# The rank-16 product of the log decay: two fp32 passes over 16 rows, or one fp32r pass over 80 stacked rows

## The chip, the cores and the metric

The kernel runs on one core of a Trainium2 chip. The metric is device time in microseconds (us) of one execution; the time before is the median of three runs. The core has a matrix engine (PE, with its weight loads shown as PEld), a vector engine (DVE), an activation engine (ACT), a general engine (POOL) and a queue that issues DMAs (SP). Each works through its own instructions in order, and semaphores tie them together.

## What is computed

One encoder block over 16 meta tokens and 1024 sequence tokens with 1024 channels, in float32. A norm is followed by one wide projection, whose columns are split into eight parts. Two mixers run beside each other: a pooling mixer, and gated linear attention (GLA) with 4 heads in chunks of 64 tokens. Their outputs are weighted by sigmoid gates, summed and projected, and a squared-ReLU MLP and a last norm follow. What matters here is the log decay of GLA:

```python
z = jnp.einsum('bld,dn->bln', u, w_in)
a, q, k, v, r, lr, ga, gb = jnp.split(z, IN_SPLITS, axis=-1)
log_a = jax.nn.log_sigmoid((lr @ w_gate_up + b_gate).astype(jnp.float32)) / GLA_TAU
...
b = jnp.cumsum(ac, axis=2)
decay = jnp.exp(-jnp.abs(b[:, :, :, None, :] - b[:, :, None, :, :]))
scores = jnp.einsum('bhtk,bhsk,bhtsk->bhts', qc, kc, decay)
```

`lr @ w_gate_up` is a product of rank 16: for every token 16 numbers times a 16 x 256 matrix. The 256 results are the decay of 4 heads with 64 channels each.

## The kernel before, in words

**Number formats.** Large products are made from fp32r operands. Each float32 operand is split into a high part, made by an ACT copy into fp32r, and a low part, made by subtracting the high part on DVE or POOL. Three matrix passes then give high by high, high by low and low by high (`mm3`, lines 246 to 248). Small products take float32 operands as they are, and the PE runs each as two passes. The product of the log decay (`log_decay`, line 1073) is one of these.

**Stages.** (1) From the start to about 200 us: norm, transposes, the tile `lrtok` with the 16 columns of `lr` by token, and the gates in quarter blocks (`start`, `differences`, `gate_stage`). (2) To about 305 us: the pooling mixer, which ends with four `ya_block` steps that read the tile `pm` and write to `ma_dram`. (3) From 305 us: `gla_open` lays out the tiles of GLA, then `gla` runs. (4) From about 490 us: the outputs of GLA are merged and projected. (5) From about 630 us: the MLP, and the last norms with the output.

**The 16 columns.** `lr_turn` (line 508) turns `lrtok` on the PE: the meta tokens go to `lrT_meta` (16 x 16), the sequence to the first 16 rows of `gB` (16 x 1024). It is called in stage 1, between blocks that split the operands of the gates (`halved`, lines 708 and 709; `differ`, line 714). There the order on ACT, DVE and POOL is the program's. The weight `wgu` (16 x 256) is fetched at line 775 in stage 1.

**GLA.** Four units are worked on, (p, half) = (0,0), (1,0), (0,1), (1,1): a pair of heads by 512 tokens. Each unit begins in `inside` with `log_decay`: the product, then on ACT a bias, `Abs`, `Exp` and `Ln` in the tile `yt`, then one DVE instruction that writes `g`, and an `Exp` on `g` (line 1140). Then come seven groups of small score products (`scores`, line 1128); six of them follow a level of growing factors (`grow`, lines 1158 to 1162) and are taken into `scc` under a mask (line 1189). `across` follows one unit behind and ends with lines 1257 to 1260, which read the tile `mix`, of which `g` is a quarter. `meta_state` makes a `log_decay` of 16 tokens for p = 0 and for p = 1, just ahead of the units (0,0) and (1,0). Between these pieces the PE is given filler work: the k columns (`k_block`, evacuated at line 958), the second half of v, the rest of the gates gb, and the GLA output product.

**What sets the order.** The PE's order is the program's, everywhere. On ACT, DVE, POOL and SP a planner sets the order within the stages, by its own estimate of when things are ready, except in stage 1 and from the end of GLA into stage 4 (`in_order`), where ACT and DVE follow the program. Weights come through a ring (`Ring.top_up`): a DMA into a raw tile (line 101), the high part on ACT (line 77), the low part (line 78) on DVE, and on POOL during GLA.

**Memory.** Tiles are pushed onto two stacks, left and right. A new tile that takes the place of an old one waits until the old one's last reader is done. At `gla_open` the right stack keeps only its lowest tile (`vw1`, line 797); `pm` lay next above it.

Of the kernel before, what the change touches and what calls it, by code (L numbers as in the profile page):

```python
# [8 lines left out]
F32 = mybir.dt.float32  # L9
F32R = mybir.dt.float32r  # L10
U8 = mybir.dt.uint8
ACT = mybir.ActivationFunctionType
ALU = mybir.AluOpType
AX = mybir.AxisListType

P = 128
# [4 lines left out]
HALF = 512  # L21
# [84 lines left out]
def kernel(  # L106
# [3 lines left out]
    nc = tc.nc  # L110
# [3 lines left out]
    w_gate_up, b_gate, gla_norm, w_gla_out, w_out = w_gate_up[0], b_gate[0], gla_norm[0], w_gla_out[0], w_out[0]  # L114
    norm_ffn, w_ff1, w_ff2 = norm_ffn[0], w_ff1[0], w_ff2[0]

    act, dve, pool, pe = nc.scalar, nc.vector, nc.gpsimd, nc.tensor
    left, right = Stack(tc, "left"), Stack(tc, "right")
# [19 lines left out]
    def bank(tag):  # L138
        if tag in rota:
            turn_of[tag] = turn_of.get(tag, -1) + 1  # L140
            tag = rota[tag][turn_of[tag] % len(rota[tag])]
        return psp[tag].tile([P, 512], F32, name=f"b_{tag}", tag=tag)
# [20 lines left out]
    gB = left.push("gB", [P, D], F32)  # L163
# [10 lines left out]
    stat = [tiny(16) for _ in range(4)]  # L174
    eps_t = tiny(1)
    pool.memset(eps_t, EPS)
    wgu = left.push("wgu", [16, 256], F32)
    metab = left.push("metab", [P, 4, 16], F32)
    lrT_meta = left.push("lrT_meta", [16, 32], F32)[:, :16]
    raw = Raw(nc, [left.push(f"raw{i}", [P, D], F32) for i in range(2)])  # L180
    W1 = Ring(nc, raw, left.push("w1h", [P, 2, D], F32R), left.push("w1l", [P, 2, D], F32R), 2)
    left_ff = left.mark()
# [8 lines left out]
    def f32(ap):  # L191
        return ap.bitcast(F32)

    def col(v, n):
        return v.rearrange("(h p) -> p h", p=P)
# [54 lines left out]
    def quad(a):  # L250
        return a.rearrange("p (k c) -> p k c", k=4)
# [149 lines left out]
    S, rings = {}, [W1]  # L401
# [32 lines left out]
    def buffer(key, depth, size=HALF):  # L434
        S[key] = left.push(key, [P, depth, size], F32)
        S["n" + key], S["d" + key] = 0, depth
# [36 lines left out]
    def v_tile(i, t, later=False):  # L473
# [25 lines left out]
        def leave_lr():  # L499
            if i == 0:  # L500
                act.activation(S["lrtok"][:n, t], b[:, 256:], ACT.Copy)
# [3 lines left out]
        leave()  # L505
        leave_lr()

    def lr_turn():
        b = bank("ms")
        pe.transpose(b[:16, :16], S["lrtok"][:16, 8], ident[:16, :16])  # L510
        act.activation(lrT_meta, b[:16, :16], ACT.Copy)
        for h in range(2):
            b = bank("ms")
            for t in range(4):
                pe.transpose(b[:16, t * P : (t + 1) * P], S["lrtok"][:, 4 * h + t], ident)
            act.activation(gB[:16, h * HALF : (h + 1) * HALF], b[:16], ACT.Copy)
# [248 lines left out]
    def gate_stage():  # L765
        q = gate_quarters
        S["u3p"] = right.push("u3p", [P, 2, HALF], F32)
        buffer("t1", 3)
        buffer("o", 2)
        buffer("c", 2)  # L770
        q.room = True
        nc.sync.dma_start(pscale, col(pool_scale, 4))
        nc.sync.dma_start(bgate, col(b_gate, 2))
        nc.sync.dma_start(gnorm, col(gla_norm, 4))
        nc.sync.dma_start(wgu, w_gate_up)
        q.leaving = next_weights
        for _ in S["gate_run"]:
            pass
        rota["mm"] = ("mm", "mm", "x", "x")
# [7 lines left out]
    one = []  # L787
    step(one, start)
    step(one, gate_stage)


# [134 lines left out]
    def gla_open():  # L926
        raw.back()
        W1.eng = pool
        right.pop_to(1)
        left.pop_to(left0)  # L930
        S["kq"] = [left.push(f"kq{h}", [P, 2, 2, HALF + OFF[h]], F32) for h in range(2)]
        for h in range(2):
            q = S["kq"][h][:, :, 1, OFF[h] : OFF[h] + HALF]
            for p in range(2):
                nc.sync.dma_start(q[:, p], q_dram[p, h])
        S["v"].append(left.push("v1", [P, NC, 2 * P], F32))
        buffer("t1", 3)
        buffer("o", 3)

        mix = left.push("mix", [P, 4, HALF], F32)  # L940
        S["kt"], S["qe"], S["kl"], S["g"] = quad(mix[:, 0]), mix[:, 1], mix[:, 2], mix[:, 3]
        S["on"], S["sr"] = mix[:, 0:2].rearrange("p a (b c) -> p (a b) c", b=4), mix[:, 2:4]
        S["ends"] = left.push("ends", [P, HALF], F32)
        S["scc"] = left.push("scc", [P, 2, 2, 4, CH], F32)
        S["S"] = left.push("S", [P, 2, 2, P], F32)
        S["W"] = left.push("W", [P, NC - 1, P], F32)
        S["left_n"] = left.mark()
        S["N"] = [left.push(f"n{i}", [P, HALF, 2], F32) for i in range(2)]
        S["F"] = left.push("f", [P, HALF, 2], F32)
        S["yt"] = left.push("yt", [P, 2, HALF], F32)  # L950
        banks(keep=1, sc=1, m2=1, mx=1, ms=1)
        rota["mm"] = ("mm", "mm", "mx")

    step(one, gla_open)

    def k_block(p):
# [110 lines left out]
        step(fill, yb_block(j, 0), W1, [rows4(w_gla_out, j)])  # L1067


    def log_decay(lrT, p, n, dst, y, t, tag="ms"):  # L1070

        b = bank(tag)[:, :n]
        pe.matmul(b, wgu[:, p * P : (p + 1) * P], lrT, start=True, stop=True)
        act.activation(y, b, ACT.Identity, bias=bgate[:, p : p + 1])
        act.activation(t, y, ACT.Abs)
        act.activation(t, t, ACT.Exp, scale=-1.0)
        act.activation(t, t, ACT.Ln, bias=1.0)
        dve.scalar_tensor_tensor(dst, y, 0.0, t, ALU.min, ALU.subtract)
# [52 lines left out]
    def inside(p, half, before):  # L1131

        kq = S["kq"][half][:, p, :, OFF[half] : OFF[half] + HALF]
        N, F, scc, g, ends = S["N"], S["F"], S["scc"][:, p], S["g"], S["ends"]
        log_decay(gB[:16, half * HALF : (half + 1) * HALF], p, HALF, g, S["yt"][:, 0], S["yt"][:, 1])
        act.activation(g, g, ACT.Exp, scale=1.0 / TAU)  # L1140
        yield 4.5
        b = scores(kq[:, 0], kq[:, 1])
        act.activation(scc, b, ACT.Copy)
        pairs = lambda a: a.rearrange("p (b u) n -> p b u n", u=2)
        plain, gp = kq.rearrange("p n (b u) -> p b u n", u=2), g.rearrange("p (b u) -> p b u", u=2)
        for u, to, other in ((1, N[0], F), (0, F, N[0])):
            dve.tensor_tensor(
                pairs(to)[:, :, u], plain[:, :, u], gp[:, :, u : u + 1].broadcast_to([P, HALF // 2, 2]), ALU.mult
            )
            act.activation(pairs(other)[:, :, u], plain[:, :, u], ACT.Copy)  # L1150

        def grow(m, n, to, e, e2):

            b = HALF // (4 * m)
            outer = lambda a: bass.AP(a.tensor, a.offset, (a.ap[0], (8 * m, b), (6 * m, 2), (1, 2 * m)))
            inner = lambda a: bass.AP(a.tensor, a.offset + 2 * m, (a.ap[0], (8 * m, b), (2 * m, 2), (1, 2 * m)))
            over = lambda at, step: bass.AP(e.tensor, e.offset + at, (e.ap[0], (4, b), (step, 2), (0, 2 * m)))
            dve.tensor_tensor(outer(to), outer(n), over(1, 1), ALU.mult)
            act.activation(inner(to), inner(F), ACT.Copy)
            dve.tensor_tensor(inner(F), inner(n), over(0, 3), ALU.mult)  # L1160
            ev = e.rearrange("p (b u) -> p b u", u=2)
            dve.tensor_tensor(e2, ev[:, :, 0], ev[:, :, 1], ALU.mult)

        def last(n, e, e2):

            m = CH // 2
            ev = e.rearrange("p (b u) -> p b u", u=2)
            halves_of = lambda a: a.rearrange("p (b u m) -> p b u m", u=2, m=m)
            for i, o, u in ((0, S["kl"], 0), (1, S["qe"], 1)):
                a, f, o = halves_of(n[:, :, i]), halves_of(F[:, :, i]), halves_of(o)  # L1170
                dve.tensor_tensor(o[:, :, u], a[:, :, u], ev[:, :, 1 - u : 2 - u].broadcast_to([P, NC, m]), ALU.mult)
                act.activation(o[:, :, 1 - u], f[:, :, 1 - u], ACT.Copy)
            dve.tensor_tensor(e2, ev[:, :, 0], ev[:, :, 1], ALU.mult)

        yield 2.0
        e, at = g, 0
        for lvl in range(6):
            m, n = 1 << lvl, N[lvl % 2]
            to = at + HALF // (2 * m)
            e2 = ends[:, at:to]  # L1180
            if lvl < 5:
                grow(m, n, N[1 - lvl % 2], e, e2)
            else:
                while before and before not in done:
                    yield 0.8
                last(n, e, e2)
            e, at = e2, to
            b = scores(n[:, :, 0], n[:, :, 1])
            dve.copy_predicated(scc, mask[:, lvl : lvl + 1, None, :].broadcast_to([P, 2, 4, CH]), b)
            yield LEVEL  # L1190
# [487 lines left out]
```

## Time and profile before

| what | value |
| --- | --- |
| runs shown (us) | 1247.72, 1245.71, 1245.96 |
| median | 1245.96 us |
| profiled execution | span 1247.8 us from first to last instruction |
| PE busy | 1213.1 us, 97% of the span |
| DVE, ACT, POOL busy | 850.7, 615.4, 65.0 us |
| granted PE clock | 0.993 of full |

No separate time is given for the profiled execution, so its span stands for it; it is 1.8 us (0.15%) above the median of the runs and equal to the slowest of them. In the profile's rows "L1073" is line 1073 of the kernel, the bracket at the end of a row is idle time of the engine just before the instruction and what ended it, and "x2" means that the row stands for two instructions. A float32 product shows two weight loads and two matmuls, one of each for a pass.

### The profile page before, as it was taken

What the parts mean: (1) busy time and instruction counts of PE and PEld (TensorE: products, weight loads), DVE (VectorE), ACT (ScalarE), POOL (GpSimd) and SP (SyncE); (2) the same over time, 40 slices, a digit from 0 to 9 for tenths busy, and PEclk for the clock granted to TensorE, in tenths of its full rate; (3) what the DMA queues carried; (4) which work ended last, traced back from release to release, by engine and by line L of the source; (5) the groups of instructions that cost most, each with busy time, mean ns of one, the idle gap of its engine ahead of it and who ended that gap; (6) DMA issues with size and microseconds to landing.
All of it is one profiled execution on the core that took longest, in us unless ns stands there. A gap on an engine that the chain in (4) does not pass through costs nothing.

```text
span 1247.8 us, 18255 instructions
## 1 busy us (share of the span) xinstructions
PE 1213.1 (97%) x6822; PEld 1006.5 (81%) x6822; DVE 850.7 (68%) x1384; ACT 615.4 (49%) x1092; POOL 65.0 (5%) x70
## 2 busy tenths in 40 slices
PE   7999999999999999799999999999999999999997
PEld 6878888988887788688878888888887788888886
DVE  6897676653556677723897676766774777887786
ACT  6667567321446663412654554555553444444554
POOL 2100000001101115300000000000000000000000
PEclk9999999999999999899999999999999999999999
DMA  8033326156102246831234544544569773333432
GB/s 249 2 109 104 109 85 197 52 161 204 36 19 61 86 140 223 284 104 51 94 117 155 167 152 136 164 156 135 177 219 371 267 247 94 102 93 100 162 96 90
DMA packets 142682, 173.85 MB, mean 139 GB/s; under 512 B 10969, under 2 KB 82417, under 8 KB 142593
## 3 DMA queue, kind: packets, MB, share of 16 engines
q1 hardware_dynamic: 142592, 172.68, 42.8%
q8 instruction: 54, 0.88, 0.3%
q14 instruction: 36, 0.29, 0.1%
HBM read 119.17 MB, written 53.48 MB: 138 GB/s over the span
## 4 chain that ended last, share of the span: by engine, by line
PE 90%; DVE 5%; DMA 2%; issue 1%; ACT 1%; SPq 0%; DVEq 0%; ACTq 0%
PE b_mm L246 11%; PE b_mm L247 11%; PE b_mm L248 11%; PE b_ms L246 9%; PE b_ms L247 9%; PE b_ms L248 9%; PE b_x L246 8%; PE b_x L248 8%; PE b_x L247 8%; PE b_sc L1128 1%; PE b_mx L246 1%; PE b_mx L247 1%; PE b_mx L248 1%; PE b_ms L538 1%; DMA raw<-hf_dram 1%
## 5 line engine op out<-in xcount | busy, mean ns | idle before, releaser
L246 PE MATMUL b_mm<-th,w1h 128*128 128x512 f32 (+1 forms) x312 | 117.8, 378 | 3.2 <-ACT th L1385 2.1
L247 PE MATMUL b_mm<-tl,w1h 128*128 128x512 f32 (+1 forms) x312 | 116.0, 372 | 0.6 <-DVE tl L1386 0.6
L248 PE MATMUL b_mm<-th,w1l 128*128 128x512 f32 (+1 forms) x312 | 115.8, 371 | 0.0
L246 PE MATMUL b_x<-th,w1h 128*128 128x512 f32 (+1 forms) x240 | 90.8, 378 | 0.0
L247 PE MATMUL b_x<-tl,w1h 128*128 128x512 f32 (+1 forms) x240 | 90.6, 378 | 0.0
L248 PE MATMUL b_x<-th,w1l 128*128 128x512 f32 (+1 forms) x240 | 90.3, 376 | 0.0
L264 ACT ACTIVATE w1h<-raw 128x512 fp32r<-128x512 f32 x96 | 59.6, 621 | 36.7 <-PE b_x L247 14.1
L265 DVE TENSOR_TENSOR w1l<-raw,w1h 128x512 fp32r<-128x512 f32 x96 | 65.6, 684 | 12.3 <-ACT w1h L264 12.3
L246 PEld LDWEIGHTS b_mm<-th,w1h 128*128 128x128 f32 x312 | 58.5, 188 | 16.5 <-issue 3.3
L264 ACT ACTIVATE w1h<-fs 128x512 fp32r<-128x512 f32 x72 | 45.4, 631 | 46.4 <-PE b_ms L247 31.7
L247 PEld LDWEIGHTS b_mm<-tl,w1h 128*128 128x128 f32 x312 | 58.6, 188 | 10.5 <-DVE tl L1386 0.9
L248 PEld LDWEIGHTS b_mm<-th,w1l 128*128 128x128 f32 x312 | 58.6, 188 | 10.3
L264 ACT ACTIVATE w1h<-bt 128x512 fp32r<-128x512 f32 x44 | 27.8, 632 | 67.7 <-issue 59.5
L265 DVE TENSOR_TENSOR w1l<-fs,w1h 128x512 fp32r<-128x512 f32 x72 | 49.3, 685 | 14.7 <-ACT w1h L264 14.6
L1535 DVE TENSOR_TENSOR bt<-w,w 128x512 f32<-128x512 f32 x80 | 54.6, 683 | 0.4 <-DMA w<-in_w_ff_dram 0.4
L248 PEld LDWEIGHTS b_x<-th,w1l 128*128 128x128 f32 x240 | 45.1, 188 | 8.5
L246 PEld LDWEIGHTS b_x<-th,w1h 128*128 128x128 f32 x240 | 45.0, 188 | 8.4
L247 PEld LDWEIGHTS b_x<-tl,w1h 128*128 128x128 f32 x240 | 45.1, 188 | 8.2
L264 ACT ACTIVATE fxh<-bt 128x512 fp32r<-128x512 f32 x36 | 22.8, 632 | 57.6 <-issue 48.1
L246 PE MATMUL b_ms<-wo,w1h 128*128 128x512 f32 x128 | 49.8, 389 | 0.0
L247 PE MATMUL b_ms<-wo,w1h 128*128 128x512 f32 x128 | 49.8, 389 | 0.0
L248 PE MATMUL b_ms<-wo,w1l 128*128 128x512 f32 x128 | 49.8, 389 | 0.0
(438 smaller groups left out, 3370.2 us busy)
## 6 DMA issues: line engine op xcount, KB each, us to landing
hf_dram<-h SPq DMA_DIRECT2D x112, 256.0 KB, 2.1
raw<-hf_dram SPq DMA_DIRECT2D x112, 256.0 KB, 2.6
w<-in_w_ff_dram SPq DMA_DIRECT2D x64, 256.0 KB, 4.8
raw<-in_w_in_dram SPq DMA_DIRECT2D x24, 512.0 KB, 4.8
raw<-in_w_ff_dram SPq DMA_DIRECT2D x16, 512.0 KB, 4.1
rawx<-in_w_ff_dram SPq DMA_DIRECT2D x16, 512.0 KB, 4.0
xs<-in_x_dram SPq DMA_DIRECT2D x8, 512.0 KB, 4.9
rawx<-in_w_in_dram SPq DMA_DIRECT2D x8, 512.0 KB, 4.4
```

The lines of the kernel that those rows point to most:

```text
L246: pe.matmul(ps, ah, bh, start=first and i == 0, stop=False, skip_group_check=more)
L247: pe.matmul(ps, ah, bl, start=False, stop=False, skip_group_check=more)
L248: pe.matmul(ps, al, bh, start=False, stop=last and i == n - 1, skip_group_check=more)
L264: act.activation(hi, a, ACT.Copy)
L265: dve.tensor_tensor(lo, a, f32(hi), ALU.subtract)
L538: pe.transpose(b[j][:, i], u[:, (4 * j + i) * P : (4 * j + i + 1) * P], ident)
L1128: pe.matmul(b[to, e, j], kk[r, s], qq[r, s], start=True, stop=True, tile_position=(e * CH, u * CH))
L1535: dve.tensor_tensor(bt, w, S["w2"][q[3:]][:, i], ALU.add if q[2] == "+" else ALU.subtract)
```

## The change

The two operands of the product are stacked three times on partitions: the 16 rows of the tokens as (high, low, high) at partitions 0, 32 and 64, the 16 rows of the weight as (high, high, low) at the same partitions, and zeros on the rows between. One pass in fp32r over 80 rows then sums high by high, low by high and high by low.

```diff
-    wgu = left.push("wgu", [16, 256], F32)
+    wgu = left.push("wgu", [P, 256], F32R)
-    lrT_meta = left.push("lrT_meta", [16, 32], F32)[:, :16]
+    lrT_meta = left.push("lrT_meta", [P, 32], F32R)[:, :16]
...
+    RANK = 16
+    part_of = lambda a, i: a[32 * i : 32 * i + RANK]
+
+    def stacked(to, a, low):
+        pool.memset(f32(to[: 64 + RANK]), 0.0)
+        for i in range(3):
+            if i != low:
+                act.activation(part_of(to, i), a, ACT.Copy)
+        dve.tensor_tensor(part_of(to, low), a, f32(part_of(to, 0)), ALU.subtract)
+
     def lr_turn():
...
-        act.activation(lrT_meta, b[:16, :16], ACT.Copy)
+        stacked(lrT_meta, b[:16, :16], 1)
...
-        nc.sync.dma_start(wgu, w_gate_up)
...
         right.pop_to(1)
         left.pop_to(left0)
+        S["wgraw"] = right.push("wgraw", [RANK, 256], F32)
+        nc.sync.dma_start(S["wgraw"], w_gate_up)
+        stacked(wgu, S["wgraw"], 2)
...
-        S["yt"] = left.push("yt", [P, 2, HALF], F32)
+        S["y"] = left.push("y", [P, HALF], F32)
+        S["lr"] = left.push("lr", [P, HALF], F32R)
+        lr_of(0)
...
+    def lr_of(half):
+        stacked(S["lr"], gB[:RANK, half * HALF : (half + 1) * HALF], 1)
+
     def log_decay(lrT, p, n, dst, y, t, tag="ms"):
-        b = bank(tag)[:, :n]
-        pe.matmul(b, wgu[:, p * P : (p + 1) * P], lrT, start=True, stop=True)
+        b, k = bank(tag)[:, :n], slice(0, 64 + RANK)
+        pe.matmul(b, wgu[k, p * P : (p + 1) * P], lrT[k], start=True, stop=True)
...
-        log_decay(gB[:16, half * HALF : (half + 1) * HALF], p, HALF, g, S["yt"][:, 0], S["yt"][:, 1])
+        log_decay(S["lr"], p, HALF, g, S["y"], g)
+        if (p, half) == (1, 0):
+            lr_of(1)
```

The weight's DMA moves from stage 1 to `gla_open`, into a new tile `wgraw` on the right stack. The second half of the tokens is stacked into the same tile `lr` once unit (1,0) has read the first half. The two halves of `yt` become `y` and `lr`, and `Abs`, `Exp` and `Ln` are written into `g` itself.

## The prediction

> **What bounds the kernel now.** I read the page's chain first, then the busy time by stretches around the four units of GLA, then the order of time at each log-decay product. First the chain by engine (page), then four stretches: microseconds, and busy time of PE, PEld, DVE, ACT and POOL.
>
> ```profile
> PE 90%; DVE 5%; DMA 2%; issue 1%; ACT 1%; SPq 0%; DVEq 0%; ACTq 0%
> ```
>
> ```profile
> 305.00:317.00 12.00, 12.00 (x77) 10.92 (x76) 1.92 (x2) 3.71 (x6) 0.00 (x0) 1.00 0.15 57
> 317.00:345.00 28.00, 27.06 (x370) 23.26 (x372) 17.50 (x39) 14.30 (x29) 4.78 (x2) 1.00 0.16 40
> 345.00:375.00 30.00, 29.23 (x442) 25.95 (x435) 17.07 (x45) 11.33 (x26) 0.00 (x0) 1.00 0.07 20
> 388.00:428.00 40.00, 40.00 (x457) 31.24 (x456) 26.81 (x50) 27.05 (x46) 7.17 (x3) 1.00 0.29 87
> ```
>
> The PE is the path that sets the end for 90% of the span, and where the four products stand (317, 348, 388 and 428 us) it rests for 0.94 us of 28, 0.77 of 30 and nothing of 40. DVE and ACT are busy for 38 to 68% there. So a microsecond of PE work removed here should be a microsecond of the span, as long as nothing new makes the PE wait.
>
> **What the change removes: PE time.** The order of time on the PE around the product at 317 us (with the meta product ahead of it) and the one at 388 us; then the first and last row around those at 348 and 428 us; then, from the chain in order of time, eight narrow passes of an earlier stage.
>
> ```profile
> 316.92 0.28 PE L247 MATMUL b_mm<-tl,w1h 128*128 128x264 f32 x1
> 317.04 0.28 PE L248 MATMUL b_mm<-th,w1l 128*128 128x264 f32 x1
> 317.25 0.39 PE L1073 MATMUL b_mx<-lrT_meta,wgu 16*128 16x16 f32 x2
> 317.50 1.10 PE L1073 MATMUL b_ms<-gB,wgu 16*128 16x512 f32 x2
> 318.53 0.39 PE L246 MATMUL b_mm<-th,w1h 128*128 128x264 f32 x1
> 318.75 0.28 PE L247 MATMUL b_mm<-tl,w1h 128*128 128x264 f32 x1
> ```
>
> ```profile
> 387.68 0.39 PE L247 MATMUL b_mm<-tl,w1h 128*128 128x512 f32 x1
> 387.92 0.40 PE L248 MATMUL b_mm<-th,w1l 128*128 128x512 f32 x1
> 388.24 1.12 PE L1073 MATMUL b_ms<-gB,wgu 16*128 16x512 f32 x2
> 389.29 0.50 PE L246 MATMUL b_mm<-th,w1h 128*128 128x512 f32 x1
> 389.63 0.40 PE L247 MATMUL b_mm<-tl,w1h 128*128 128x512 f32 x1
> ```
>
> ```profile
> 348.05 0.28 PE L248 MATMUL b_mm<-vw,tl 128*128 128x256 f32 x1
> 349.75 0.28 PE L247 MATMUL b_mm<-vw,th 128*128 128x256 f32 x1
> ```
>
> ```profile
> 427.54 0.39 PE L248 MATMUL b_mx<-th,w1l 128*128 128x512 f32 x1
> 429.25 0.40 PE L247 MATMUL b_mx<-tl,w1h 128*128 128x512 f32 x1
> ```
>
> ```profile
> 48.16 0.59 PE b_ms L693 x8
> ```
>
> The reader should look at starts, since the ends of matmuls are modelled and overlap. An fp32r pass of 512 columns takes 387.92 - 387.68 = 0.24 us from start to start, one of 264 columns 317.04 - 316.92 = 0.12. The two fp32 passes over 512 columns hold the PE for 389.29 - 388.24 = 1.05 us, and 0.08 us go on entering (388.24 - 387.92 less 0.24) and 0.10 on leaving (389.63 - 389.29 less 0.24).
>
> From the last pass before to the second pass after, the four places take 1.71, 1.70, 1.71 and 1.71 us. With one pass each the same stretch is made of ordinary steps. At 388 and 428 us that is three of 0.24 = 0.72, so 0.99 us is saved at each. At 317 and 348 us it is two of 0.12, one of 0.24, and the meta pass of 16 columns. No row shows that pass in fp32r; it lies between 0.07 us (0.59 / 8, passes with 16 columns or rows at 48 us) and the 0.12 us of 264 columns. I take 0.1, since the weight load is as wide as theirs. That is 0.58 us, and 1.13 and 1.12 us are saved. The sum is 1.13 + 1.12 + 0.99 + 0.99 = **4.2 us**.
>
> Its lower bound keeps the entering and leaving at all four places, 4 x 0.18 = 0.7 us less: 3.5 us. Upwards only 0.06 us is to be had. [...] The trace has no 80-row product that would decide.
>
> **What it adds: stage 1.** Rows of the old copies (ACT), of the smallest two-input DVE group, of the stretch behind `lr_turn`, and the PE's longest wait in it.
>
> ```profile
> L511 ACT ACTIVATE lrT_meta<-b_ms x1: 156/156/156, 61.1 to 61.1; 16x16 f32<-16x16 f32 x1
> ```
>
> ```profile
> L516 ACT ACTIVATE gB<-b_ms x2: 570/570/571, 61.1 to 61.6; 16x512 f32<-16x512 f32 x2
> ```
>
> ```profile
> L1089 DVE TENSOR_TENSOR metab<-metab x8: 164/167/169, 321.2 to 352.1; 128x8 f32<-128x8 f32 x8
> ```
>
> ```profile
> 70.00:85.00 15.00, 12.20 (x53) 9.45 (x52) 13.91 (x21) 10.59 (x19) 0.00 (x0) 1.00 0.39 105
> ```
>
> ```profile
> PE b_ms L248 <- DVE w1l L265: 1.7, 1, 1.7
> ```
>
> Stacking the meta columns adds one ACT copy (0.16 us), one small POOL clear, and one DVE subtraction, which I size at 0.17 us by the 128x8 row. POOL does nothing in this stretch and ACT has 4.4 us of 15 free, so those two are hidden. DVE is busy for 13.9 us of 15 and the PE waits for it, in program order, so its 0.17 us goes on the path: **+0.2 us**. Unhidden, the ACT copy would make it 0.4. The removed DMA of 16 KB was an entry on SP that nobody waited for: 0.
>
> **What it adds: the stacks for GLA.** Rows of ACT, POOL and SP around `gla_open`, what SP waited for, and the landing time of the old weight DMA.
>
> ```profile
> 305.45 1.06 ACT L77 ACTIVATE w1h<-raw 128x1024 fp32r<-128x1024 f32 x1 [9.72 <-PE b_x L247]
> ```
>
> ```profile
> 317.91 2.38 POOL L78 TENSOR_TENSOR w1l<-raw,w1h 128x1024 fp32r<-128x1024 f32 x1 [20.65 <-ACT w1h L77]
> ```
>
> ```profile
> 299.71 7.01 SPq L904 DMA_DIRECT2D ma_dram<-o  x4
> 320.31 0.38 SPq L101 DMA_DIRECT2D raw<-in_w_in_dram  x1
> ```
>
> ```profile
> SPq L101 <- POOL w1l L78: 13.5, 1, 13.5
> ```
>
> ```profile
> DMA to landing us min/median/max: 4.2/4.2/4.2
> ```
>
> The stack of the first half needs only `gB`, ready at 62 us: one clear, two ACT copies of 0.57 us and one DVE subtraction. ACT is idle for 9.72 us before 305.45, so it is hidden. The weight is the tight one. Its tile lies where `pm` was, so its DMA waits for the last PE pass of `ya_block`, at 305.4 us. On SP it goes out at the latest behind the last `ma_dram` write, 299.71 + 7.01 = 306.7 us, with 0.4 us for its issue; it lands 4.2 us later, at 311.3. Two copies (at most 0.57 each) and a subtraction (at most 0.82, a 512-wide DVE row below) give 313.3 us. The PE comes to it at 317.25 - 0.2 us. So 3.7 us are in hand: 0 on the path. SP's next entry, L101, stands waiting from 306.7 to 320.3 anyway, so a DMA ahead of it delays nobody.
>
> The second stack, behind unit (1,0)'s product at 348 us, adds one clear on POOL (at most half of the 2.38 us row, which is twice as wide and has two inputs), 2 x 0.57 us on ACT and up to 0.82 us on DVE, at worst all ahead of the unit's own `Exp` and first DVE work: 2.0 us behind schedule, or 3.2 with the clear. What hides it is the time until the PE uses that unit's factors. The rows are the DVE's on masks and factors, and the PE's from the chain:
>
> ```profile
> 340.02 0.73 DVE L1189 COPY_PREDICATED scc<-mask,b_sc 128x512 f32<-128x512 uint8 x1 [1.75 <-PE b_sc L1128]
> ...
> 345.36 0.74 DVE L1189 COPY_PREDICATED scc<-mask,b_sc 128x512 f32<-128x512 uint8 x1 [2.14 <-PE b_sc L1128]
> ...
> 354.48 0.81 DVE L1147 TENSOR_TENSOR f<-kq,mix 128x512 f32<-128x512 f32 x1
> ```
>
> ```profile
> 395.65 0.81 DVE L1147 TENSOR_TENSOR f<-kq,mix 128x512 f32<-128x512 f32 x1
> ```
>
> ```profile
> 360.82 0.48 PE b_sc L1128 x32
> ...
> 399.48 0.48 PE b_sc L1128 x31
> ```
>
> In unit (1,0) the factors are written by 355.3 us and the first masked scores run at 360.8: 5.5 us in hand against 3.2. Writing `Abs` into `g` instead of `yt` adds no wait: `g` was last read by the `across` of an earlier unit, which has ended before the last level of the unit just done.
>
> **The sum.** -4.2 + 0.2 + 0 = -4.0 us. The profiled span of 1247.8 us would become 1243.8; the median of the runs, 1245.96 us, lies 1.8 us below that span, and the forecast stands against it: **1242.0 us**, 0.32% faster. About 0.2% (2.5 us) is what can be told from no change here. By the lower bound (3.5) and the unhidden copy (0.4) it is 1242.9; by the upper (4.3, and 0.2) 1241.9. Runs before spread over 2.0 us, so the forecast's own range is 1240.5 to 1244.0.
>
> **Rivals.**
>
> (B) The gain is half absorbed, because ACT and DVE do not come earlier with the PE where they are busy with filler work at the product (ACT is busy for 27 us of 40 from 388 us on). If the PE meets late factors in two of the four units, about 2.0 us is lost: 1244.0 us, no change by the bound. Against it: DVE itself waited for the PE's scores for 1.75 and 2.14 us late in unit (0,0), so there the PE is the late one by more than the 1.1 us it gains; in unit (0,1) the factors are written at 396.5 and used at 399.5, 3.0 us in hand against 1.0.
>
> (C) The slower side: the weight's DMA is put behind the waiting L101 on SP. That queue works in order and stood on this entry for 13.5 us. Then it is issued at 320.7 us, lands at 324.9, and with 2.0 us for copies and subtraction is ready at 326.9. The PE, whose order is fixed, stands at its first meta product from 317.1 on: 9.8 us lost, 1245.96 - 4.0 + 9.8 = 1251.8 us. It decides from a readiness of 317.1 + 4.0 + 2.5 = 323.6 us on. For it: the planner does order loads ahead, L101 among them. Against: the tile is free 15 us before the raw tile that L101 wants, and the weight comes first in the program.
>
> (D) The planner orders ACT, DVE and SP anew all the way to the end, since its own clock has shifted. The PE's waits show what such an order is worth:
>
> ```profile
> PE b_mm L246 <- ACT wo L1324: 4.6, 2, 4.1
> ```
>
> One more wait of that length is 4.1 us: 1246.1 us, no change. For it: the order there rests on the planner's estimates. Against: most of what follows 490 us starts from the PE and would shift as a whole.
>
> **How the numbers follow.** Forecast 0.62, B 0.14, C 0.16, D 0.08. C carries any lateness of the stacks that costs over 6.5 us. Faster has the forecast's 0.62, same B and D, 0.22, slower C, 0.16. The range runs from 1240.2 us (the forecast less the runs' spread) over B and D to 1246.8 us (D and its spread); what it leaves out is C and the tails.
>
> **What would show it.** Right: one PE row of L1073 per product, "80*128", spaced 0.24 us from its neighbours (4.2), or with 0.2 us around it (3.5); starts at 430 us about 4 us earlier; one DVE row of about 0.17 us at 65 us; SP's `wgraw` row near 306 us. Wrong: a wait of the PE at the product for DVE or ACT (C); more than 1.7 us of PE idle time between 317 and 375 us (B); unchanged gains at 430 us but not at 630 us (D).

## The result, and the profile after

| | before | changed |
| --- | --- | --- |
| median of 22 runs each | 1246.29 us | 1243.95 us |
| lowest and highest | 1243.67 to 1249.09 | 1241.63 to 1247.97 |
| ratio, 95% interval | | 0.9982 [0.9974, 0.9990] |

The changed kernel is 0.18% faster, 2.3 us, and by the interval between 1.2 and 3.2 us. The forecast was 4.0 us; both ranges that the prediction gives held the time, the narrower one by 0.05 us, and about two fifths of the forecast gain are missing.

Line numbers have moved: the product of `log_decay` is now line 1092, the chain of the meta decays 1097, 1107, 1108 and 1117 with its transpose on the PE at 1120, the scores 1147, the factors 1168, `grow` 1179 to 1183, the mask 1210, the state 1242, the output products 1249, and `stacked` 514 to 518.

First the chain by engine from the page of the changed kernel, then three of the four stretches shown of before (busy us of PE, PEld, DVE, ACT and POOL), then the PE's waits between 317 and 460 us (total, times, longest).

```profile
PE 85%; DVE 8%; ACT 3%; DMA 2%; issue 2%; SPq 0%; DVEq 0%; ACTq 0%
```

```profile
317.00:345.00 28.00, 27.06 (x383) 24.09 (x382) 18.31 (x40) 13.46 (x29) 4.79 (x2) 1.00 0.15 40
345.00:375.00 30.00, 28.66 (x417) 25.57 (x416) 18.64 (x51) 12.75 (x28) 0.52 (x1) 1.00 0.12 37
388.00:428.00 40.00, 38.37 (x453) 30.83 (x452) 27.77 (x51) 26.40 (x45) 5.73 (x3) 1.00 0.29 87
```

```profile
PE b_m L1249 <- DVE S L1242: 1.6, 1, 1.6
...
PE b_mx L1120 <- DVE metab L1117: 0.8, 1, 0.8
PE b_m L1249 <- DVE W L1242: 0.2, 1, 0.2
```

The chain goes over DVE for 8% in place of 5%. The PE rested for 0.77 us of the 30 from 345 us on, now for 1.34; it rested for nothing of the 40 from 388 us on, now for 1.63. None of the three waits shown is there before. None is at the product itself: they are at the meta state, 7 us behind the second product, and at the GLA state, 18 us behind the third.

**The PE time that was removed.** The order of time on the PE in the changed kernel, around the product at 317 us and the one at 388 us.

```profile
316.32 0.28 PE L248 MATMUL b_mm<-th,w1l 128*128 128x264 f32 x1
316.44 0.18 PE L1092 MATMUL b_mx<-lrT_meta,wgu 80*128 80x16 f32 x1
316.48 0.48 PE L1092 MATMUL b_ms<-lr,wgu 80*128 80x512 f32 x1
316.79 0.29 PE L246 MATMUL b_mm<-th,w1h 128*128 128x264 f32 x1
316.92 0.28 PE L247 MATMUL b_mm<-tl,w1h 128*128 128x264 f32 x1
```

```profile
385.94 0.40 PE L248 MATMUL b_mm<-th,w1l 128*128 128x512 f32 x1
386.17 0.39 PE L1092 MATMUL b_ms<-lr,wgu 80*128 80x512 f32 x1
386.40 0.40 PE L246 MATMUL b_mm<-th,w1h 128*128 128x512 f32 x1
386.63 0.39 PE L247 MATMUL b_mm<-tl,w1h 128*128 128x512 f32 x1
```

At 386 us the 80-row pass holds the PE for 0.23 us, like its neighbours, with nothing for entering or leaving. The four stretches from the last pass before to the second pass after take 0.60, 0.58, 0.69 and 0.70 us where they took 1.71, 1.70, 1.71 and 1.71: 4.26 us less. The product starts 0.04 us behind the meta pass, but it then holds the PE for 0.31 us (316.79 - 316.48) where the one at 386 us holds it for 0.23; so the meta pass costs 0.12 us in all.

**Where it came back.** Two profiles have different starting points, so a later row is read against an earlier one. The ACT copies of stage 1 and of 200 us, and the one that ends unit work at 460 us, first before, then changed:

```profile
66.55 0.61 ACT L264 ACTIVATE w1h<-s 128x512 fp32r<-128x512 f32 x1
...
74.01 0.63 ACT L264 ACTIVATE w1h<-raw 128x512 fp32r<-128x512 f32 x1
...
200.64 0.63 ACT L859 ACTIVATE t<-c 128x512 f32<-128x512 f32 x1
...
461.09 1.06 ACT L1259 ACTIVATE yg<-mix 128x1024 fp32r<-128x1024 f32 x1
```

```profile
65.60 0.62 ACT L264 ACTIVATE w1h<-s 128x512 fp32r<-128x512 f32 x1
...
73.35 0.62 ACT L264 ACTIVATE w1h<-raw 128x512 fp32r<-128x512 f32 x1
...
199.96 0.63 ACT L870 ACTIVATE t<-c 128x512 f32<-128x512 f32 x1
...
459.01 1.06 ACT L1280 ACTIVATE yg<-mix 128x1024 fp32r<-128x1024 f32 x1
```

The changed kernel's profile begins 0.95 us ahead (65.60 - 66.55). At 74 us it is 0.66 ahead and at 200 us 0.68: stage 1 costs 0.3 us. At 461 us it is 2.08 ahead, so GLA has brought 2.08 - 0.68 = 1.4 us where 4.26 us of PE work went. Two places take 2.9 us of it.

*The meta state at unit (1,0).* DVE and PE in the changed kernel, then before:

```profile
350.62 0.68 DVE L518 TENSOR_TENSOR lr<-gB,lr 16x512 fp32r<-16x512 f32 x1
...
351.62 0.81 DVE L1168 TENSOR_TENSOR n<-kq,mix 128x512 f32<-128x512 f32 x1
...
352.32 0.28 PE L248 MATMUL b_mm<-vw,tl 128*128 128x256 f32 x1
...
352.43 0.80 DVE L1168 TENSOR_TENSOR f<-kq,mix 128x512 f32<-128x512 f32 x1
...
353.21 0.17 DVE L1117 TENSOR_TENSOR metab<-metab,kq 128x16 f32<-128x16 f32 x1
...
353.44 0.28 PE L1120 MATMUL b_mx<-ident,metab 128*16 128x128 f32 x1 [0.83 <-DVE metab L1117]
353.74 0.52 PE L1228 MATMUL b_ms<-ident,mix 128*128 128x128 f32 x3
```

```profile
352.96 0.17 DVE L1098 TENSOR_TENSOR metab<-metab,kq 128x16 f32<-128x16 f32 x1
...
355.26 0.28 PE L248 MATMUL b_mm<-vw,tl 128*128 128x256 f32 x1
355.38 0.27 PE L1101 MATMUL b_mx<-ident,metab 128*16 128x128 f32 x1
355.49 0.60 PE L1207 MATMUL b_ms<-ident,mix 128*128 128x128 f32 x4
```

Before, the small meta chain on DVE ended 2.25 us ahead of the PE's transpose that wants it (355.38 less 352.96 + 0.17). In the changed kernel the PE comes 2.26 us earlier against the row at 200 us (352.32 + 0.12 = 352.44, less 355.38, plus 0.68), and the chain ends 0.93 later (353.21 - 352.96 + 0.68): the new subtraction L518 stands in it, and both 512-wide factor instructions L1168, which came behind it before. From the last filler pass to the second instruction after it the PE takes 1.42 us where it took 0.23: 1.19 us are lost.

*The state in unit (0,1).* POOL, DVE and PE in the changed kernel, then before:

```profile
400.26 2.41 POOL L78 TENSOR_TENSOR w1l<-raw,w1h 128x1024 fp32r<-128x1024 f32 x1 [11.34 <-ACT w1h L77]
...
400.45 2.77 DVE L1181 TENSOR_TENSOR f<-n,ends 128x512 f32<-128x512 f32 x1
...
402.36 0.39 PE L248 MATMUL b_mx<-th,w1l 128*128 128x512 f32 x1
...
403.89 0.35 DVE L1242 SCALAR_TENSOR_TENSOR S<-W,ends,b_m 128x128 f32<-128x128 f32 x1
...
404.39 0.87 PE L1249 MATMUL b_m<-v,scc 64*64 64x128 f32 x12 [1.63 <-DVE S L1242]
```

```profile
402.31 0.69 DVE L1160 TENSOR_TENSOR f<-n,ends 128x512 f32<-128x512 f32 x1
...
403.22 2.40 POOL L78 TENSOR_TENSOR w1l<-raw,w1h 128x1024 fp32r<-128x1024 f32 x1 [12.40 <-ACT w1h L77]
...
405.33 0.39 PE L248 MATMUL b_mx<-th,w1l 128*128 128x512 f32 x1
405.65 1.53 PE L1228 MATMUL b_m<-v,scc 64*64 64x128 f32 x24
```

The same DVE instruction takes 2.77 us in place of 0.69. Before, it had ended at 403.00, 0.22 us ahead of POOL's low part; now POOL starts 0.19 us ahead of it. By the profile POOL's instruction came 2.96 us earlier, as the PE's row at 402.36 did (2.97), and the DVE's only 1.86. The state `S` behind it is late, and the PE loses 2.03 - 0.32 = 1.71 us between these two of its rows.

Together that is 1.19 + 1.71 = 2.90 us, and 4.26 - 2.90 = 1.36 us is left, against the 1.4 read above. Two smaller steps nearly cancel: the wait of 0.2 us at 445 us, and a wait for `scc` that lasted 0.68 us before (at 373.79 us) and lasts 0.40 now. Less the 0.3 of stage 1, 1.1 us arrives at 460 us.

That POOL holds up DVE is not new. The kernel before shows it on two instructions of this size (0.68 us elsewhere), in unit (0,0) at 333.30 us (2.53 us) and in unit (1,1) at 435.72 us (2.90 us), each time just behind the start of a low part on POOL (332.89 and 435.23). The first of them:

```profile
333.30 2.53 DVE L1158 TENSOR_TENSOR n<-n,ends 128x512 f32<-128x512 f32 x1
```

No wait of the PE came of either: the only one between 317 and 345 us, 0.94 us, is as long in e8 (0.9 us), where POOL makes none of these low parts, and between 428 and 460 us there is none. New is that the hold-up falls on an instruction ahead of the state that the PE wants next.

After 490 us single profiles tell nothing of the change: two profiles of the kernel before drift 3.9 us apart from there to the end. Nor do the whole spans. Where time and span of one execution are both on record, the time is 1.7 to 3.1 us longer; if that holds for the profiled execution of before, whose time is not on record, its span of 1247.8 us stands for about 1249.5 us or more (an estimate), longer than any of the 22 runs, while that of the changed kernel, 1241.63 us, is the shortest of its 22. Whether the 2.3 us of the runs are the 1.1 us of 460 us, at the near end of their interval, or more, stays open.

### The profile page after: what moved, and what is told of

It reads as the page before. It is cut to its first block, busy times and chain, and to the rows that moved or that the text cites. A ratio compares the mean times of both kernels' runs of the same rounds, so it can differ in the third digit from the quotient of the medians.

```text
span 1239.6 us, 18265 instructions
## 1 busy us (share of the span) xinstructions
PE 1206.1 (97%) x6816; PEld 1003.1 (81%) x6816; DVE 850.9 (69%) x1388; ACT 618.8 (50%) x1099; POOL 66.6 (5%) x74
## 4 chain that ended last, share of the span: by engine, by line
PE 85%; DVE 8%; ACT 3%; DMA 2%; issue 2%; SPq 0%; DVEq 0%; ACTq 0%
PE b_mm L246 10%; PE b_mm L247 10%; PE b_mm L248 10%; PE b_ms L247 9%; PE b_ms L246 9%; PE b_ms L248 9%; PE b_x L248 8%; PE b_x L246 8%; PE b_x L247 8%; PE b_sc L1147 1%; PE b_ms L550 1%; PE b_mx L246 1%; PE b_m L1249 1%; PE b_mx L247 1%; PE b_mx L248 1%
```

## The experiments

Two theories stood. The first: the gain is lost where work that does not move with the PE gets in its way, namely the new DVE work ahead of the meta state, and POOL's low part beside a two-input DVE instruction. Its rival: the planner has arranged ACT, DVE and POOL anew, and the waits come from its order. Diffs are against the changed kernel. As a measure I give how many us an ACT row stands ahead of before, each against its own row at 200 us: the copy of v at 364 us (behind two products and the meta state), and the copies `yg` at 421 us (behind the third product and the state) and at 461 us (behind the fourth).

| kernel | 364 us | 421 us | 461 us | median us | ratio to before, same group |
| --- | --- | --- | --- | --- | --- |
| changed | 1.04 | 0.59 | 1.40 | 1243.95 | 0.9982 [0.9974, 0.9990] |
| e9_after | 1.02 | 0.58 | 1.33 | 1244.32 | 0.9983 [0.9970, 0.9995] |
| e6_null | 0.04 | 0.04 | 0.06 | 1247.69 | 1.0010 [0.9997, 1.0024] |
| e1_later | 1.71 | 1.28 | 2.06 | 1243.22 | 0.9946 [0.9928, 0.9963] |
| e2_port | 1.12 | 2.39 | 3.16 | 1244.50 | 0.9956 [0.9938, 0.9974] |
| e4_pass16 | 1.48 | 2.40 | 3.08 | 1244.39 | 0.9952 [0.9934, 0.9971] |
| e5_stacks_only | 0.00 | 0.29 | 0.36 | 1246.11 | 0.9978 [0.9963, 0.9994] |
| e7_later_dve4 | 1.70 | 2.32 | 3.10 | 1242.36 | 0.9971 [0.9957, 0.9984] |
| e8_later_dve | 1.73 | 2.34 | 3.42 | 1245.55 | 0.9986 [0.9974, 0.9998] |
| e10_meta_late | 1.67 | 2.29 | 3.06 | 1241.72 | 0.9961 [0.9948, 0.9974] |
| e11_again | 1.72 | 2.36 | 3.17 | 1242.56 | 0.9963 [0.9951, 0.9975] |

Traces of one kernel agree within 0.1 us here, times only within 0.1 to 0.2%. So causes are read from the traces, and the times say no more than their intervals. The kernels were run in groups, each with its own runs of before: e1, e2, e4 and e5 (before 1248.54), e6 to e9 (1247.31), e10 and e11 (1246.85). In the first group the ratios of e1, e2 and e4 stand for 5.5 to 6.7 us, more than the 4.26 us of PE time that there was to win, so ratios of different groups are not compared.

**e1_later: the second stack later in the program.**

```diff
         log_decay(S["lr"], p, HALF, g, S["y"], g)
-        if (p, half) == (1, 0):
-            lr_of(1)
...
             dve.copy_predicated(scc, mask[...], b)
+            if (p, half, lvl) == (1, 0, 4):
+                lr_of(1)
             yield LEVEL
```

> The second stack is made three us-scale steps later, after the fifth of the six levels of unit (1,0), instead of right behind its log-decay product; nothing else differs from the changed kernel. Theory 1 (the second stack delayed the DVE work of the meta state, for which the PE waited 0.8 us at the transpose of line 1120, and in unit (0,1) a POOL subtraction held a DVE instruction for 2.1 us because the PE's own gain moved POOL's work against DVE's): the wait at that transpose is gone (0.8 to 1.0 us of PE time comes back between 349 and 360 us), the collision in unit (0,1) stays or moves; time 0.5 to 1.0 us under the changed kernel, about 1243.0. Rival (the planner's new order as a whole, not the stack's place, cost the 2.3 us): the wait stays, time as the changed kernel, about 1244.0.

One row of the PE's waits and one of the DVE's order of time:

```profile
PE b_mx L1120 <- DVE metab L1117: 0.3, 1, 0.3
```

```profile
351.28 0.68 DVE L518 TENSOR_TENSOR lr<-gB,lr 16x512 fp32r<-16x512 f32 x1
```

The wait falls from 0.8 to 0.3 us and 0.67 us come back at 364 us. But the subtraction has not moved: the planner still puts it into the meta chain, at 351.28. What moved is one of the two factor instructions, which now runs behind the chain. So what stands in the meta chain on DVE is the cause, as the first theory has it, and much of that is the planner's doing, as its rival has it: each is right in part. The collision in unit (0,1) is still there, and what was won at 364 us arrives unchanged at 421 and 461 us.

**e2_port: POOL's fourth low part in GLA as a clear.**

```diff
-            self.eng.tensor_tensor(lo, raw, hi.bitcast(F32), ALU.subtract)
+            self.lows = getattr(self, "lows", 0) + (self.eng is self.nc.gpsimd)
+            if self.eng is self.nc.gpsimd and self.lows == 4:
+                self.eng.memset(lo.bitcast(F32), 0.0)
+            else:
+                self.eng.tensor_tensor(lo, raw, hi.bitcast(F32), ALU.subtract)
```

> The changed kernel with one POOL instruction exchanged: the low part of the fourth weight block that POOL splits during GLA (the one that runs beside unit (0,1) at 400 us) is not computed but cleared to zero by POOL, so that this instruction writes and does not read; the low part of that block is left out of the gate. Theory 1: the DVE instruction at line 1181 that took 2.77 us beside it takes 0.7 us, the PE's wait of 1.6 us for the state at line 1242 is gone, and the time is 1.6 to 1.8 us under the changed kernel, about 1242.3. Rival (the wait comes from the order on DVE, not from POOL): DVE's 2.77 us falls, but the wait and the time stay, about 1244.0.

POOL and DVE at the same place, in order of time:

```profile
400.43 0.97 POOL L80 MEMSET w1l<- 128x1024 f32 x1 [10.44 <-PE b_mm L252]
...
400.64 0.68 DVE L1183 TENSOR_TENSOR n<-n,ends 128x512 f32<-128x512 f32 x1
...
401.50 0.68 DVE L1185 TENSOR_TENSOR f<-n,ends 128x512 f32<-128x512 f32 x1
```

With POOL only writing, the two-input DVE instruction that runs inside POOL's keeps its 0.68 us. It is not the one that was held up: that one (line 1185 here) now runs just behind the clear, which is shorter and starts earlier, and takes 0.68 us too. The PE's wait for `S` is gone, and 1.8 us come back at 421 us. The meta wait of 0.8 us is as it was. So the two-input DVE instruction of 128x512 that starts just behind POOL's took 2.77 us beside the subtraction (changed kernel) and 0.68 us beside the clear. Beside the subtraction it ended 0.55 us after POOL's end at 402.67; the two held up in the kernel before ended 0.54 us (333.30 + 2.53 against 332.89 + 2.40) and 0.58 us (435.72 + 2.90 against 435.23 + 2.81) after POOL's.

**e4_pass16: one fp32r pass over 16 rows.**

```diff
-        pool.memset(f32(to[: 64 + RANK]), 0.0)
         for i in range(3):
-            if i != low:
+            if i == 0:
                 act.activation(part_of(to, i), a, ACT.Copy)
-        dve.tensor_tensor(part_of(to, low), a, f32(part_of(to, 0)), ALU.subtract)
...
-        b, k = bank(tag)[:, :n], slice(0, 64 + RANK)
+        b, k = bank(tag)[:, :n], slice(0, RANK)
```

> The pass alone: one fp32r pass over the 16 high rows of tokens and weight, without clears, second copies and subtractions; the two products with low parts are left out of the log decay. One ACT copy per operand remains. If the PE's saving is the whole story and the stacks cost the rest, the PE row is as short as with 80 rows (0.23 us from start to start), the wait at the meta transpose is gone, and the time is 4.0 us under the kernel before, about 1242.2. Theory 1 expects the collision of POOL and DVE in unit (0,1) to stay, since it comes from the gain itself: 2.3 to 3.2 us under the kernel before, about 1243.5. If a 16-row pass pays an entry and an exit that the 80-row pass does not, 0.2 us per product are missing.

The PE's order of time around the third product:

```profile
386.43 0.40 PE L248 MATMUL b_mm<-th,w1l 128*128 128x512 f32 x1
386.76 0.49 PE L1090 MATMUL b_ms<-lr,wgu 16*128 16x512 f32 x1
387.18 0.50 PE L246 MATMUL b_mm<-th,w1h 128*128 128x512 f32 x1
387.51 0.40 PE L247 MATMUL b_mm<-tl,w1h 128*128 128x512 f32 x1
```

The stretch takes 1.08 us with 16 rows against 0.69 with 80, of the same columns and format: the 16 rows take 0.39 us more, 0.10 ahead of the pass (386.76 - 386.43 less 0.23), 0.19 in it (387.18 - 386.76 less 0.23) and 0.10 behind it (387.51 - 387.18 less 0.23). So of the 1.02 us saved at this product (1.71 - 0.69), 0.63 come with the single fp32r pass and 0.39 with the 80 rows. This is the question that the prediction left open between 4.2 and 3.5 us. The price of 0.39 us is larger than the 0.18 us (0.08 and 0.10) read from the float32 passes. Why 16 rows pay it and 80 do not is not shown.

This kernel has neither new wait: no subtraction stands in the meta chain, and in unit (0,1) POOL starts 0.17 us behind the DVE instruction (401.11 against 400.94), which keeps its 0.68 us, while POOL takes 2.78 us. The first theory expected the collision to stay. Which of the two waits is a matter of tenths of a microsecond. The subtraction was not all that stood in the meta chain: from its first start to its last end the chain lasts 2.67 us before, 3.08 here, 3.66 in e1 and 4.25 in the changed kernel. By these differences (an estimate, since the kernels also differ in when the PE comes) one factor instruction adds 0.4 us, the subtraction 0.6 and the other factor instruction 0.6.

The four stretches are 2.74 us shorter than before, and 3.08 us arrive at 461 us: about 0.3 us come from the wait for `scc` at 374 us, 0.42 us here in place of 0.68.

**e5_stacks_only: all stacks, the product in two float32 passes.**

```diff
-        pe.matmul(b, wgu[k, p * P : (p + 1) * P], lrT[k], start=True, stop=True)
+        k = slice(0, RANK)
+        pe.matmul(b, f32(wgu[k, p * P : (p + 1) * P]), f32(lrT[k]), start=True, stop=True)
```

> The stacks alone: all clears, copies and subtractions of the changed kernel, but the product as two fp32 passes over the 16 high rows, as long as the kernel before has them; the products with low parts are left out of the log decay. Theory 1: the wait at the meta transpose is there (0.8 to 1.0 us), stage 1 pays 0.2 us, the collision in unit (0,1) is gone with the gain: 0.5 to 1.3 us over the kernel before, about 1247.2. Rival (the stacks are free and all that was lost was lost to the gain's collisions): as the kernel before, 1246.3.

The last instruction of the meta chain, and the transpose that wants it:

```profile
353.59 0.18 DVE L1118 TENSOR_TENSOR metab<-metab,kq 128x16 f32<-128x16 f32 x1
...
355.92 0.27 PE L1121 MATMUL b_mx<-ident,metab 128*16 128x128 f32 x1
```

The first theory expected a wait of 0.8 to 1.0 us here, and there is none: the stacks alone leave 2.15 us in hand at the meta state, with the subtraction in its chain, and cost the PE nothing in GLA (0.00 us at 364, 0.36 ahead at 461). So the meta wait needs both, the added work and a PE that comes earlier. In unit (0,1) POOL starts at 403.49 us, 0.24 us behind the end of the DVE instruction, as it did before: without the earlier PE there is no collision. The time, 0.22% under before, is not explained by the trace, which has 0.3 us lost in stage 1 and 0.36 won in GLA; the runs of before in that group spread over 9 us.

**e6_null and e9_after: the two kernels once more, in the second group.**

> The kernel before, unchanged, against itself: ratio 1.000. How far it strays from 1 is what a ratio of this study can mean; above all it tells whether the 0.22% of the stacks-only kernel, whose traces show 0.4 us by the end of GLA, can be chance.

> The changed kernel again, on the chip of this group: 0.998 of before by its first measurement; 2.2 to 2.6 us. By the traces 1.9 us are gained by the end of GLA and nothing is expected to be added or lost after it.

The kernel before strays by 0.1% from itself in time and by 0.06 us in the trace up to 461 us. The changed kernel shows the same three waits (1.6, 0.8 and 0.2 us) and the same time, so these are no accidents of one profile. The 1.9 us of the expectation were read at the copy `yg` of 493 us, where the two profiles of before differ by 0.6 us; at 461 us it is 1.3 to 1.4.

**e7_later_dve4: as e1, and that one low part on DVE.**

```diff
+            self.lows = getattr(self, "lows", 0) + (self.eng is self.nc.gpsimd)
+            eng = self.nc.vector if self.eng is self.nc.gpsimd and self.lows == 4 else self.eng
-            self.eng.tensor_tensor(lo, raw, hi.bitcast(F32), ALU.subtract)
+            eng.tensor_tensor(lo, raw, hi.bitcast(F32), ALU.subtract)
```

> The whole computation, with the second stack made after the fifth level of unit (1,0), and the low part of the fourth weight block that POOL splits in GLA made by DVE instead. Theory 1: both known losses are gone, so that the units (1,0) and (0,1) keep 3.0 us or more of the 4.2 by the time the third unit's output is scaled, less up to 0.5 us for 1.23 us more DVE work; about 1243.3 against 1246.3 of before. Rival (DVE is what binds in unit (0,1), however it is loaded): a wait of the PE for the states at line 1242 stays at over 1 us, and the time is that of the changed kernel.

> The kernel with the later second stack and one block's low part on DVE, a second time: 0.997 of the kernel before, as the first time, 1.2 to 1.5 us under the changed kernel; by the trace 3.1 us ahead of the kernel before when the third unit's output is scaled.

The longest of the PE's waits that is new against before:

```profile
PE b_m L1251 <- DVE S L1244: 0.6, 1, 0.6
```

The low part takes 1.22 us on DVE, the instruction that was held up takes 0.68 us again, and the wait for `S` falls from 1.6 to 0.6 us. 3.1 us of the 4.26 arrive at 461 us in place of 1.4. e11 is the same kernel again and agrees within 0.1 us in the trace.

**e8_later_dve: as e1, and all low parts of GLA on DVE.**

```diff
-        W1.eng = pool
```

> The whole computation, with the second stack made later as in the kernel before this one, and all low parts of the weights of GLA made by DVE, none by POOL: no such instruction of POOL is left beside DVE (those of line 1065 stay). [...] If DVE's load binds, the PE waits for DVE grow and the time is above the changed kernel.

The DVE instruction of unit (1,1) that took 2.90 us in the kernel before takes 0.68 us here (line 1176, at 433.38 us), and up to 461 us e8 is as good as e7 (3.42 us ahead). But in the last unit a new wait appears, from the PE's waits between 460 and 500 us:

```profile
PE b_m L1276 <- DVE mix L1272: 1.2, 1, 1.2
```

At the copy `yg` of 493 us only 1.3 us of the gain are left, where e7 has 3.7 (two profiles of before differ by 0.6 us at this row). e8's median, 1245.55 us, is above the changed kernel's in the same group (1244.32), which was expected if DVE's load binds, though the intervals overlap. By the traces, POOL is better left with the low parts, all but the one that collides.

**e10_meta_late: as e7, and the meta columns stacked at `gla_open` in the program.**

```diff
+    lrT_raw = metab[:16, 0]
...
-        stacked(lrT_meta, b[:16, :16], 1)
+        act.activation(lrT_raw, b[:16, :16], ACT.Copy)
...
         stacked(wgu, S["wgraw"], 2)
+        stacked(lrT_meta, lrT_raw, 1)
```

> As the kernel with the later second stack and one block's low part on DVE, and the stack of the meta columns is made in gla_open beside that of the weight, from a plain copy kept in a tile, instead of in lr_turn. Theory: stage 1 pays the DVE subtraction in full (0.30 us between 57 and 63 us in every kernel that has it there, 0.0 in the one without); without it the PE comes 0.3 us earlier to GLA and everything after is as in that kernel: 0.3 us less by the trace, too little for the times to show. Rival: stage 1 absorbs it later anyway, and the start of GLA against 50 us is as in the other kernels.

The second of the two ACT rows of stage 1:

```profile
72.93 0.63 ACT L267 ACTIVATE w1h<-raw 128x512 fp32r<-128x512 f32 x1
```

It stands 1.08 us ahead of before, as the first one does (65.47 us), so stage 1 costs nothing now, and GLA is as in e7. The trace does not show the stack at `gla_open`, though: the two copies run at 61.0 and 61.2 us and the subtraction at 89.9 us (0.17 us), still in stage 1. So the 0.3 us hang on the place of the subtraction at 64.6 us, and the extra copies on ACT cost nothing. The kernel's median of 1241.72 us is the lowest of all, 0.39% under before [0.26, 0.52]. That it is faster than the kernel before is measured; that it is faster than the changed kernel rests on the traces (0.3 us in stage 1, 1.7 us by 461 us), since the intervals of the ratios overlap.

## Why the prediction was right in its sign and half wrong in its size

- **PE time removed: right.** Forecast 4.2 us, found 4.26. The steps of 0.24 us stand as drawn (0.23 found). The choice of 4.2 over 3.5, that 80 rows enter and leave free, was the author's estimate, which no row of before shows; the changed kernel shows it (0.23 us to and from the pass at 386 us), and e4 shows that 16 rows cost 0.39 us more than 80. The meta pass was taken at 0.1 us and costs 0.12.
- **Stage 1: the right place, a little small.** Forecast 0.2 us, found 0.3. The subtraction lasts 0.16 us, but from the start of the instruction ahead of it (line 726, 62.24 us) to the one behind (64.80) it is 2.56 us where it was 2.27, so it took 0.29 us of this full row. e10, where it runs 25 us later, pays nothing.
- **The weight stack: right, the working too careful.** DMA row and subtraction row of the weight, from the group views of their tile:

```profile
L943 SPq DMA_DIRECT2D wgraw<-in_w_gate_up_dram x1: 332/332/332, 304.9 to 304.9; - x1
...
L518 DVE TENSOR_TENSOR wgu<-wgraw,wgu x1: 417/417/417, 307.8 to 307.8; 16x256 fp32r<-16x256 f32 x1
```

  It was ready at 308.2 us, 8.2 us before the PE came at 316.4, where 3.7 were forecast: SP issued it ahead of the last `ma_dram` write, and it landed in 1.5 us where 4.2 were taken. Rival C did not occur.
- **The second stack at nothing: this step failed.** The prediction put its 2.0 to 3.2 us against the 5.5 us until the unit's own factors are used. That cover held. But the same DVE serves the meta state of p = 1 at that moment, and there only 2.25 us were in hand, which the PE's own gain of 2.26 us used up; the chain ended 0.93 us later, and 1.19 us were lost. The subtraction is the smaller part of it: of the 1.6 us by which the chain got longer, about 0.6 are its own, and the planner's two factor instructions are the rest (the estimate under e4). Asked for was "what hides it", and only one of the two users was asked.
- **"A microsecond of PE work is a microsecond of the span, as long as nothing new makes the PE wait": the condition failed.** The prediction looked for DVE and ACT being late at the products. It never asked what a PE that comes earlier does to POOL. POOL's low part follows the PE through the weight ring (2.96 us earlier, and the PE 2.97), the DVE's factors follow it less (1.86), and with a distance of 0.22 us between them a shift of 1.1 us put one on top of the other: 1.71 us. e2 and e7 show it: with POOL only writing, or that low part on DVE, it is gone. That POOL can hold up DVE stood in the rows of before (333.30 and 435.72 us); what a shift of POOL against DVE would do was not asked.
- **Rival B** (half absorbed, 1244.0 us) is nearest to what came, in size and in its sign: the PE rests for 2.28 us between 317 and 375 us, and over 1.7 were named. But the kernel before rests there for 0.94 + 0.77 = 1.71 us already, so this sign could not tell much. Its mechanism did not occur: no unit met late factors; the PE met a late meta state and a late GLA state. It was priced as one place doubled, at a chance of 0.14.
- **The sign "starts at 430 us about 4 us earlier" was wrong.** The second pass behind the fourth product starts at 426.98 where it started at 429.25; less the 0.95 us between the profiles, that is 1.3 us.
- **Rival D** cannot be judged after 490 us. Inside GLA the planner did set DVE's order anew, and it has part in the meta wait (e1); it has none that is shown in the collision.
- **The ranges.** 1240.5 to 1244.0 and 1240.2 to 1246.8 us both stand in the prediction, and its terms give neither: 1242.0 with the runs' spread of 2.0 us is 1240.0 to 1244.0, and rival D with it ends at 1248.1. That the time lies 0.05 us inside the narrower one is luck; the two waits are in no term of it.
- **The size.** 0.18% lies just inside the 0.2% that the prediction called the limit, and its interval reaches over it. Of the 4.0 us forecast, 1.1 were there at 460 us; the 2.9 us between are the two waits. That the runs gained 2.3 us, more than those 1.1, is not explained.

## What to carry to other kernels

An engine that gets faster moves everything that follows it, and leaves where it was what does not: before a gain is booked, list for each later meeting of two engines how much is in hand, and compare it with the gain that has piled up by then. Here 2.25 us in hand met 2.26 us of gain, and a distance of 0.22 us met a shift of 1.1. Of a piece of work on a shared engine, ask for all whom it delays, the small chains above all, and not only the one it was made for.

## What the runs showed of the hardware that was not expected

- A POOL subtraction of 128x1024 (2.41 us) held up a two-input DVE instruction that began 0.19 us after it from 0.69 to 2.77 us; where DVE began 0.17 us first, DVE kept 0.68 us and POOL took 2.78. A POOL clear of the same tile (0.97 us) held up nothing. Two hold-ups of this kind, of 2.53 and 2.90 us in the kernel before, left no wait of the PE behind them.
- A product over 16 rows between passes of 128 rows costs 0.39 us more than one over 80 rows (1.08 against 0.69 us for the stretch), at the same 512 columns in fp32r.
- An 80-row pass over 16 columns starts 0.04 us ahead of an 80-row product of 512 columns, which then holds the PE for 0.31 us in place of 0.23: together 0.12 us more.
- A DMA of 16 KB landed in 1.5 us at 305 us; the same weight's DMA took 4.2 us in stage 1 of the kernel before.
